# Making the first tile's products one by one, and loading the later weights behind the second input tile

## The chip, the core and the metric

The kernel runs on one core of a Trainium2 chip. The metric is the device time of one execution in microseconds (us). TensorE has no part in this kernel. VectorE (DVE in the profile) makes all products, ScalarE (ACT) issues the loads from its queue, SyncE (SP) issues the stores from its own, and 16 DMA engines move the bytes between HBM and the on-chip memory (SBUF).

## What is computed

Each of 16 x 1024 tokens has a row of 512 numbers and two weights. The output holds the row twice, once times each weight:

```python
batch, seq, hidden = 16, 1024, 512      # k = 2, all float32
x_expanded = x[:, :, np.newaxis, :].repeat(k, axis=2)
weights = expert_weights[..., np.newaxis]
return (x_expanded * weights).astype(np.float32)
```

`expert_indices` is not used. 33.6 MB are read and 67.1 MB are written.

## The kernel before

The 16384 tokens are dealt to 128 partitions, 128 tokens to each. They are cut into tiles of 12 tokens per partition (ten of them, in five groups of two) and a last tile of 8. A full tile is 3.15 MB of input and 6.29 MB of output. Within a group each partition's tokens are consecutive in memory, so a tile's row per partition is one run of 24 KB in and 48 KB out.

*Buffers.* Four input tiles (`XB = 4`) and two output tiles (`bufs=2`) rotate. All weights of the core sit in one tile, `w_tile`, 256 numbers per partition.

*Loads* are issued on ScalarE's queue by `load(i)` (line 80). Tiles 0 to 3 are issued before the main loop, and tile `i + 4` after tile `i` has been worked on (line 129); that load waits until the products that read the buffer are done. Tile 0 comes in three pieces of 4 tokens (line 86). Behind the first piece the weights of the first group are loaded (`first_weights`, line 56); behind the third, all the others (`other_weights`, line 59): one load for groups 1 to 4, cut into 512 runs of 192 bytes, and one for the last group, 128 runs of 64 bytes. Tiles 0 and 1 belong to the first group; tile 2 is the first to need the other weights.

*Products* (line 109) are made on VectorE 4 tokens at a time (`CH = 4`): one `tensor_tensor` multiply of 128 x 4096, with the input broadcast over the two weights and the weights broadcast over the 512 columns. A full tile takes three of them. There are 32 in all.

*Stores* (line 125) are issued on SyncE's queue, one for each tile, when the tile's last product is done. An output buffer is free again when the store two tiles back has landed. There are 11, numbered 0 to 10 below.

A framework orders the instructions and sets the semaphores. Each queue issues in program order.

Of the kernel before, what the change touches and what calls it, by code (L numbers as in the profile page):

```python
# [1 line left out]

# [4 lines left out]


@with_exitstack
def kernel(  # L10
    ctx: ExitStack,
    tc: tile.TileContext,
    x: bass.AP,
    expert_indices: bass.AP,
    expert_weights: bass.AP,
    out: bass.AP,
):
    nc = tc.nc

    batch, seq, hidden = x.shape  # L20
    k = expert_weights.shape[-1]
    P = nc.NUM_PARTITIONS
    ntok = batch * seq
    assert ntok % P == 0
    A_TOTAL = ntok // P

    f32 = mybir.dt.float32
    row = k * hidden
    TX = 12
    TO = 12  # L30
    XB = 4
    CH = 4

    groups = [[12, 12]] * 5 + [[8]]
    assert sum(sum(g) for g in groups) == A_TOTAL

    xf = x.rearrange("b s h -> (b s) h")
    of = out.rearrange("b s k h -> (b s) (k h)")
    wf = expert_weights.rearrange("b s k -> (b s) k")

    w_pool = ctx.enter_context(tc.tile_pool(name="w_pool", bufs=1))
    x_pool = ctx.enter_context(tc.tile_pool(name="x_pool", bufs=XB))
    o_pool = ctx.enter_context(tc.tile_pool(name="o_pool", bufs=2))

    w_tile = w_pool.tile([P, A_TOTAL * k], f32)

    def rows(of_all, done, T):
        return of_all[done * P : (done + T) * P, :].rearrange(
            "(p a) n -> p (a n)", a=T
        )  # L50

    T0 = sum(groups[0])
    G = len([g for g in groups[1:] if sum(g) == T0])
    head = (1 + G) * T0

    def first_weights():
        nc.scalar.dma_start(out=w_tile[:, : T0 * k], in_=rows(wf, 0, T0))

    def other_weights():
        nc.scalar.dma_start(  # L60
            out=w_tile[:, T0 * k : head * k].rearrange("p (g n) -> p g n", g=G),
            in_=wf[T0 * P : head * P, :].rearrange("(g p a) n -> p g (a n)", g=G, p=P),
        )
        nc.scalar.dma_start(
            out=w_tile[:, head * k :], in_=rows(wf, head, A_TOTAL - head)
        )

    tiles = []
    done = 0
    for group in groups:  # L70
        T = sum(group)
        a0 = 0
        for n in group:
            tiles.append((done, T, a0, n))
            a0 += n
        done += T

    loaded = []

    def load(i):  # L80
        if i >= len(tiles):
            return
        done, T, a0, n = tiles[i]
        x_tile = x_pool.tile([P, TX * hidden], f32)
        src = rows(xf, done, T)
        step = TX // 3 if i == 0 else n
        for at in range(0, n, step):
            nc.scalar.dma_start(  # L88
                out=x_tile[:, at * hidden : (at + step) * hidden],
                in_=src[:, (a0 + at) * hidden : (a0 + at + step) * hidden],  # L90
            )
            if i == 0 and at == 0:
                first_weights()
        if i == 0:
            other_weights()
        loaded.append(x_tile)

    for i in range(XB):
        load(i)
    for i, (done, T, a0, n) in enumerate(tiles):  # L100
        x_tile = loaded[i]
        outr = rows(of, done, T)
        for t in range(n):
            if t % TO == 0:
                o_tile = o_pool.tile([P, TO * row], f32)
            if t % CH == 0:
                c = (done + a0 + t) * k
                o = t % TO * row
                nc.vector.tensor_tensor(  # L109
                    out=o_tile[:, o : o + CH * row].rearrange(  # L110
                        "p (t k h) -> p t k h", t=CH, k=k
                    ),
                    in0=x_tile[:, t * hidden : (t + CH) * hidden]
                    .rearrange("p (t h) -> p t h", t=CH)
                    .unsqueeze(2)
                    .to_broadcast([P, CH, k, hidden]),
                    in1=w_tile[:, c : c + CH * k]
                    .rearrange("p (t k) -> p t k", t=CH)
                    .unsqueeze(3)
                    .to_broadcast([P, CH, k, hidden]),  # L120
                    op=mybir.AluOpType.mult,
                )
            if (t + 1) % TO == 0 or t + 1 == n:
                at = t // TO * TO
                nc.sync.dma_start(
                    out=outr[:, (a0 + at) * row : (a0 + t + 1) * row],
                    in_=o_tile[:, : (t + 1 - at) * row],
                )
        load(i + XB)

# [1 line left out]
_INS = ['x', 'expert_indices', 'expert_weights']  # L132
_OUTS = [((16, 1024, 2, 512), 'float32')]


# [23 lines left out]
```

## Time and profile before

| | |
|---|---|
| median of 3 runs | 240.62 us (239.81 to 242.09) |
| the profiled execution | 241.65 us, of which its span is 239.9 us |
| VectorE busy | 139.6 us in 32 products, 4420 ns each on average |
| first load issued, first store issued | 0.73 us, 18.87 us |
| last store issued | 223.67 us |
| a store, from issue to landing | 15.3 to 35.4 us, median 30.5 |
| a tile's load, from issue to landing | median 63.4 us for nine of the full tiles |

How to read it: the profile is one execution. Times count from the start of its span. q1 is the ring of SyncE's queue (stores), q10 that of ScalarE's (loads). A DMA's time "to landing" runs from its issue to the signal that all of its bytes are there, so it includes the time in which it waits behind others in its ring. A share of DMA is that of 16 engines' time; in a short stretch it can show over 1.00, since a packet counts where it starts. A chain of waits is followed back from the last instruction: each step names what released the next.

### The profile page before, as it was taken

Reading aid. Unit: us, or ns where it says so; the run is one execution under the profiler, and the core shown is the slowest. Engines: PE = TensorE matmul, PEld = TensorE weight load, DVE = VectorE, ACT = ScalarE, POOL = GpSimd, SP = SyncE. Lnnn points to the kernel's source line nnn. Section 1 sums busy time; section 2 is a strip of 40 time slices with the busy share of each in tenths; the row PEclk is TensorE's granted clock in tenths of the full one; section 3 lists DMA queues with packets and bytes.
Section 4 is the critical chain, followed back from the end, with each engine's and each line's share of the span. In section 5 each row is a group of like instructions: output and inputs, shape, how many; then the busy total and the mean of one; then the engine's idle time right before and its main releaser. Section 6 shows DMA issues by size and latency. Waiting matters only on the chain.

```text
span 239.9 us, 132 instructions
## 1 busy us (share of the span) xinstructions
DVE 139.6 (58%) x32; POOL 0.2 (0%) x4
## 2 busy tenths in 40 slices
DVE  0999930397079419904970794199049709939200
POOL 0000000000000000000000000000000000000000
DMA  7999999999999999999999999999999999999894
GB/s 254 424 455 365 479 410 406 459 443 389 443 410 512 393 459 393 402 516 393 410 426 418 434 475 393 459 418 467 426 426 410 448 393 481 404 459 459 383 426 186
DMA packets 4272, 100.80 MB, mean 420 GB/s; under 512 B 1200, under 2 KB 1200, under 8 KB 1200
## 3 DMA queue, kind: packets, MB, share of 16 engines
q1 hardware_dynamic: 1584, 67.11, 64.8%
q10 hardware_dynamic: 2688, 33.69, 33.6%
HBM read 33.69 MB, written 67.11 MB: 420 GB/s over the span
## 4 chain that ended last, share of the span: by engine, by line
DMA 61%; DVE 29%; DVEq 2%; issue 0%; ACTq 0%
DMA out_dram<-o_tile 60%; DVE o_tile L109 29%; DMA w_tile<-in_expert_weights_dram 2%; DVEq L154 2%; ACTq L88 0%; DVEq L109 0%
## 5 line engine op out<-in xcount | busy, mean ns | idle before, releaser
L109 DVE TENSOR_TENSOR o_tile<-x_tile,w_tile 128x4096 f32<-128x4096 f32 x32 | 139.6, 4420 | 84.0 <-DMA out_dram<-o_tile 78.3
L143 POOL MEMSET const-bfloat16-1.0<- 128x1 bf16 x1 | 0.1, 102 | 0.0
L143 POOL MEMSET const-uint8-127<- 128x1 uint8 x1 | 0.1, 102 | 0.0
L143 POOL MEMSET const-float32-0.0<- 128x1 f32 x1 | 0.1, 99 | 0.2 <-issue 0.2
L143 POOL MEMSET const-float32-1.0<- 128x1 f32 x1 | 0.1, 99 | 0.0
## 6 DMA issues: line engine op xcount, KB each, us to landing
out_dram<-o_tile SPq DMA_DIRECT2D x10, 6144.0 KB, 30.5
x_tile<-in_x_dram ACTq DMA_DIRECT2D x9, 3072.0 KB, 63.4
out_dram<-o_tile SPq DMA_DIRECT2D x1, 4096.0 KB, 15.3
x_tile<-in_x_dram ACTq DMA_DIRECT2D x3, 1024.0 KB, 6.6
x_tile<-in_x_dram ACTq DMA_DIRECT2D x1, 2048.0 KB, 61.2
w_tile<-in_expert_weights_dram ACTq DMA_DIRECT2D x1, 96.0 KB, 8.6
w_tile<-in_expert_weights_dram ACTq DMA_DIRECT2D x1, 24.0 KB, 4.5
w_tile<-in_expert_weights_dram ACTq DMA_DIRECT2D x1, 8.0 KB, 8.3
```

The costliest lines, as they stand in the source:

```text
L109: nc.vector.tensor_tensor(out=o_tile[:, o : o + CH * row].rearrange("p (t k h) -> p t k h", t=CH, k=k), in0=x_tile[:, t * hidden : (t + CH ...
L143: nc = _bacc.Bacc("TRN2", target_bir_lowering=False, num_devices=1)
L154: with _tile.TileContext(nc) as tc:
```

## The change

A new constant `SINGLES = 1` marks tile 0. For it the wide products are not made; each of its 24 products (12 tokens, two weights) is an instruction of 128 x 512 with the weight as a scalar for each partition. Those whose number leaves 2 when divided by 3, 8 of them, are made on ScalarE, the other 16 on VectorE. All other tiles are as before. And `other_weights()` is called in `load(1)` behind tile 1's load, in place of `load(0)` behind tile 0's third piece.

```diff
+    SINGLES = 1
...
-        if i == 0:
+        if i == 1:
             other_weights()
...
-            if t % CH == 0:
+            for kk in range(k if i < SINGLES else 0):
+                c = (done + a0 + t) * k + kk
+                o = t % TO * row + kk * hidden
+                if c % 3 == 2:
+                    nc.scalar.mul(
+                        out=o_tile[:, o : o + hidden],
+                        in_=x_tile[:, t * hidden : (t + 1) * hidden],
+                        mul=w_tile[:, c : c + 1],
+                    )
+                    continue
+                nc.vector.tensor_scalar(
+                    out=o_tile[:, o : o + hidden],
+                    in0=x_tile[:, t * hidden : (t + 1) * hidden],
+                    scalar1=w_tile[:, c : c + 1],
+                    scalar2=None,
+                    op0=mybir.AluOpType.mult,
+                )
+            if i >= SINGLES and t % CH == 0:
                 c = (done + a0 + t) * k
```

## The prediction

> **What bounds the kernel now.** I read the page's totals and queues first, then the DMA table by stage, then the chain that ended last, and last one steady stretch of the DMA queues.
>
> ```profile
> span 239.9 us, 132 instructions
> DVE 139.6 (58%) x32; POOL 0.2 (0%) x4
> ...
> q1 hardware_dynamic: 1584, 67.11, 64.8%
> q10 hardware_dynamic: 2688, 33.69, 33.6%
> ...
> L109 DVE TENSOR_TENSOR o_tile<-x_tile,w_tile 128x4096 f32<-128x4096 f32 x32 | 139.6, 4420 | 84.0 <-DMA out_dram<-o_tile 78.3
> ```
>
> The stores (q1) and the loads (q10) together fill 98.4% of what 16 DMA engines can carry in the span. VectorE works 58% of it and spends 78.3 us waiting for stores to land. So bytes set the end: 100.8 MB, which the change leaves alone. All that is not covered by transfers is 1.6% of 239.9, or 3.8 us. The table by stage (stretch, its length, VectorE, GpSimd, clock, DMA share, GB/s) shows where that lies:
>
> ```profile
> 0.00:2.00 2.00, 0.00 (x0) 0.20 (x4) 1.00 0.31 53
> 2.00:3.00 1.00, 0.00 (x0) 0.00 (x0) 1.00 0.68 213
> 3.00:6.00 3.00, 0.26 (x1) 0.00 (x0) 1.00 1.01 401
> 6.00:19.00 13.00, 13.00 (x4) 0.00 (x0) 1.00 1.05 437
> 19.00:32.00 13.00, 12.85 (x3) 0.00 (x0) 1.00 1.04 423
> ...
> 147.00:190.00 43.00, 26.03 (x6) 0.00 (x0) 1.00 1.00 434
> ...
> 236.00:238.00 2.00, 0.00 (x0) 0.00 (x0) 1.00 0.31 131
> 238.00:239.90 1.90, 0.00 (x0) 0.00 (x0) 1.00 0.00 0
> ```
>
> Only the first 3 us and the last 4 have free engines. From 3 to 19 us, while no store has been issued, the loads alone already fill them. The chain says the same from the other side: its links are three products (13.11 us) and then a store.
>
> ```profile
> 5.75 13.11 DVE o_tile L109 x3
> ...
> 18.87 26.60 DMA out_dram<-o_tile
> ...
> 45.60 13.11 DVE o_tile L109 x3
> ...
> 58.72 30.48 DMA out_dram<-o_tile
> ...
> 102.45 30.70 DMA out_dram<-o_tile
> ...
> 190.19 24.61 DMA out_dram<-o_tile
> ```
>
> From 58.72 to 102.45 two tiles pass, 21.87 us each; a tile is 3.15 MB in and 6.29 MB out, so 431 GB/s. At that rate a load alone takes 7.3 us and a store 14.6. A store's 30 us are mostly waiting behind the store before it. How the rings share is seen in the DMA queues from 100 to 150 us:
>
> ```profile
> q1 hardware_dynamic: 320, 14.16, 65.5%
> q10 hardware_dynamic: 320, 7.08, 33.0%
> ```
>
> They take turns packet by packet (320 against 320). A store's packet is twice as long, so stores get two thirds of the bytes.
>
> **The change, part by part.**
>
> *The two later weight loads move behind the second tile's load.* ACT's issue of tile 1 comes 0.46 + 0.59 = 1.05 us earlier (2.6 instead of 3.69). Loads 2 and 3 start at 5.49 and 5.86, long after the instruction before them ended, so they don't move. The bytes moved (0.104 MB) take 0.24 us at 431 GB/s: tile 1, which lands at 3.69 + 14.8 = 18.5, would land near 18.2. Tile 2 is the first to need these weights, at 45.6. Cost on the path: nothing, while that cover of 27 us lasts.
>
> *Tile 0's three wide products become 16 on VectorE and 8 on ScalarE.* No row shows a 512-wide product. From above: the wide row's 4418 ns / 8 = 552. From below: the 102 ns of the smallest instruction on the page. I take 552, the same work per element. ScalarE has no row at all; I bound it by 102 and twice 552 and take 552 again, nearest to the same work. The last third of tile 0 lands at 2.10 + 8.7 = 10.8. VectorE then has 5 products left: 5 x 0.552 = 2.76, so tile 0 is done at 13.6 (11.3 with the low price). ScalarE has 3: 12.5; at the double price its 8 products from 6.2 on end at 15.0. The first store is issued at about 13.6 instead of 18.87, 5.3 us earlier. The DVE time saved (13.1 - 16 x 0.552 = 4.3 us) lies beside full DMA engines.
>
> The Trainium skill, "ScalarE: Activation LUTs", section "What ACT_TABLE_LOAD costs", speaks against using ScalarE here: about 2.66 us before a first activation, then an estimated 0.7 us for each of these products. By it, an estimate, ScalarE would start products near 9 and end near 14.6, so the store would go out 1 us later than my sum has it. No run here shows it yet.
>
> *New waits.* SP's first store now waits for two engines; nothing but later stores is queued behind it. On ACT, the load of tile 4 stands behind the 8 products and also waits for VectorE; it went out at 18.88 and would go near 13.6. ACT's ring still holds tiles 1 to 3 then (they land from 18.5 to 55), so nobody waits for it. No load is queued behind the first product that was not so before: loads 0 to 3 are issued ahead of it.
>
> *What an earlier store buys.* The engines are full from 3 us on, so a store that starts 5.3 us earlier takes its bytes from loads. Tile 1 is the first to feel it: between 18.2 and, if the last 3 us of its load alternate with store packets (3 us becomes 9), about 24. Tile 1's products then end between 31.4 and 37. In this time loads 1 to 4 wait in the ring (12.6 MB, 29 us alone), so no engine runs empty. In the steady part each load lands some 11 us before VectorE asks for it (tile 4: 18.88 + 59.0 = 77.9 against 89.3). That cushion shrinks by what stores have gained: 5.3 us x 431 = 2.3 MB at most. Nothing of this shortens the sum of bytes.
>
> *The tail.* Before: store 9 is issued at 211.09 while store 8 lands at 214.80, a lead of 3.7 us; the last store is issued at 223.67 while store 9 lands at 229.3, a lead of 5.6. While both leads hold, the end stays where it is. I take 0 for this, because the last store lands 9.7 us after store 9, its bare bytes at 431, so these leads are enough.
>
> **Sum.** Head 0, products beside full DMA 0, weights 0, tail 0. The profiled execution took 241.65 (span 239.9 plus 1.75 around it), 1.03 over the median of 240.62. On the median: 240.6.
>
> **The rivals.**
>
> *A. The weights get stuck between store packets (chance 0.15).* They are 640 runs, 40 to an engine. With turns taken packet by packet, as at 320 to 320, each could wait for a 1.8 us store packet (14.6 / 8), and tile 2's load stands behind them. If store 0 comes in only as tile 1's load ends, stores 0 and 1 can pass almost alone and tile 2 lands after 50 instead of 33.6. Loads then run ahead later, stores lag, and the stores are alone earlier at the end. There the lead of store 9 falls to 14.6 - 13.25 (landing of one store to issue of the next on its buffer) = 1.4 us. A store's bytes start 0.65 us (first load: issued 0.73, 0.31 of the first 2 us) to 4 us (store 0: no packet from 18.9 to 22) after issue: price 0 to 2.6, so 240.6 to 243.2. Against it: tile 1's 13.1 us of products leave the store ring dry before store 1 comes, and small packets pass at once.
>
> The Trainium skill, "DMA: Bandwidth & Descriptors", section "Queues, rings and completion order", says an engine drains a packet of about 9 to 17 descriptors from one ring before it switches. By that the weights would pass in 3 to 5 turns, an estimated 9 us in place of up to 16 store packets (29 us).
>
> *B. Slower: the loads become the last to arrive at the end (0.13).* If the 2.3 MB that stores gained are never given back, they cost loads 2.3 / 0.144 (a third of 431) = 15.9 us. Tile 10 would land at 146.37 + 61.2 + 15.9 = 223.5 instead of 207.6, its products end at 232.3, and the last store, 9.7 us and some 1.5 of latency, lands at 243.5 instead of 238.95: 245.2. It decides from the point where tile 10 lands more than 214.9 + 5.6 - 1.5 = 219.0. Against it: a late load makes VectorE wait, the store ring runs dry, and the load then has all 431 GB/s (7.3 us instead of 21.9).
>
> *C. The change does not do what it says (0.06):* ScalarE's products take so long that store 0 goes out no earlier: 240.6.
>
> *D. Faster (0.06):* if the whole transfer ran at the 434 of the best long stretch, 100.8 MB take 232.3; with the head's 1.7 and the tail's 3.7 that is 237.7, 2.2 less than the span: 238.4 or, with the scatter of runs, below.
>
> **How the numbers follow.** The main case (0.60) and C stand at 240.6. About 1%, 2.4 us, is what a measurement of this kernel can tell from no change: 238.2 to 243.0. Same: 0.60 + 0.06 + 0.11 of A = 0.77. Slower: B 0.13 + 0.04 of A = 0.17. Faster: 0.06. The range: upwards to A's bound, 243.2; downwards by the 1.5 that the highest run lies over the median, 239.1. Left out are B and D, 0.19.
>
> **What would show it.** Right: the first store issued between 11.5 and 15; DMA share near 1.0 in every stretch from 3 to 234; loads landing later against VectorE than before; stores 9 and 10 issued ahead of the landing before them. Wrong: a stretch in which both rings are empty (A: near 213; B: VectorE waiting for tile 10 past 219), a first load issued later than 0.73, or a different rate in the steady part.

## The result and the profile after

The changed kernel takes 272.25 us (median of 4 runs, 271.97 to 273.2) against 241.11 before: a ratio of 1.130, 95% interval 1.124 to 1.137. The forecast was 240.6, in a range of 239.1 to 243.2. It was wrong by 32 us, and in kind: slower, not the same.

First the page of the changed kernel: its span, the engines' busy time, the queues and the new rows (the last columns are busy us and mean ns of one, then the idle time ahead of it and what ended that).

```profile
span 270.7 us, 155 instructions
...
DVE 133.1 (49%) x45; ACT 6.4 (2%) x9; POOL 0.2 (0%) x4
...
q1 hardware_dynamic: 1584, 67.11, 67.4%
q10 hardware_dynamic: 2688, 33.69, 29.8%
...
L127 DVE TENSOR_TENSOR o_tile<-x_tile,w_tile 128x4096 f32<-128x4096 f32 x29 | 126.6, 4422 | 115.0 <-issue 71.0
L117 DVE TENSOR_SCALAR o_tile<-x_tile,w_tile 128x512 f32<-128x512 f32 x16 | 6.5, 480 | 6.2 <-DMA w_tile<-in_expert_weights_dram 5.8
L111 ACT ACTIVATE o_tile<-x_tile,w_tile 128x512 f32<-128x512 f32 x8 | 5.1, 710 | 0.2 <-DMA x_tile<-in_x_dram 0.2
L111 ACT ACT_TABLE_LOAD x1 | 1.3, 1283 | 5.9 <-DMA x_tile<-in_x_dram 5.9
```

The bytes are the same, and the queues still fill 97.2% of 16 engines, of a span that is 30.8 us longer. So, a few us apart, the DMA engines did not wait for work. They were busy longer with the same work. The stores' ring shows where: 64.8% of 239.9 us was 155 us, 67.4% of 270.7 is 182. The loads' ring stayed at 81 us.

The timeline of the changed kernel (start, length, engine, line, operation, and in brackets the idle time before it) shows a second thing that the forecast did not have:

```profile
10.60 1.95 ACT L111 ACTIVATE o_tile<-x_tile,w_tile 128x512 f32<-128x512 f32 x3 [0.23 <-DMA x_tile<-in_x_dram]
10.60 2.07 DVE L117 TENSOR_SCALAR o_tile<-x_tile,w_tile 128x512 f32<-128x512 f32 x5 [0.36 <-DMA x_tile<-in_x_dram]
18.04 13.10 DVE L127 TENSOR_TENSOR o_tile<-x_tile,w_tile 128x4096 f32<-128x4096 f32 x3 [5.37 <-DMA x_tile<-in_x_dram]
31.16 223.50 SPq L143 DMA_DIRECT2D out_dram<-o_tile  x11
31.17 149.99 ACTq L89 DMA_DIRECT2D x_tile<-in_x_dram  x7
59.55 13.10 DVE L127 TENSOR_TENSOR o_tile<-x_tile,w_tile 128x4096 f32<-128x4096 f32 x3 [28.42 <-issue]
```

Tile 0's products are done on both engines by 12.7, 0.9 us before the forecast's 13.6. But the first store goes out at 31.16, when tile 1's products end. The built program says why (two lines of it, shortened; S[DVE_49] counts VectorE's instructions, S[Activation_49] ScalarE's). The framework put the store of tile 1 ahead of that of tile 0 in SP's queue (`out_set+12288` is tile 1's place in the output):

```
SP DMACopy wait:S[DVE_49]>=19 ...       out=[out_set+12288 ...] in=[o_tile_106_set ...]
...
SP DMACopy wait:S[Activation_49]>=8 ... out=[out_set ...]       in=[o_tile_78_set ...]
```

The trace agrees: of the two issues at 31.16 and 31.65 the first waits for VectorE's semaphore, the second for ScalarE's, whose last update before it came at 12.55. So the first two stores leave together, and with them the loads of tiles 4 and 5, at 31.17 and 31.55.

By stages (stretch, length, VectorE, ScalarE, GpSimd, clock, DMA share, GB/s) the loss of the changed kernel lies here:

```profile
36.00:216.00 180.00, 78.58 (x18) 0.00 (x0) 0.00 (x0) 1.00 1.00 366
216.00:222.00 6.00, 5.62 (x2) 0.00 (x0) 0.00 (x0) 1.00 1.04 451
222.00:234.00 12.00, 10.79 (x3) 0.00 (x0) 0.00 (x0) 1.00 0.59 254
234.00:268.00 34.00, 18.55 (x5) 0.00 (x0) 0.00 (x0) 1.00 1.01 437
```

The kernel before, without the column of ScalarE:

```profile
36.00:206.00 170.00, 99.71 (x23) 0.00 (x0) 1.00 1.00 432
```

For 180 us the engines are full (1.00) and move 366 GB/s where they moved 431 to 432 before. That stretch holds 65.9 MB, which at 431 take 152.9: 27 us lost. From 222 to 234 the share is 0.59: another 5 us of idle engines. Less the microsecond that the rest comes out ahead, this is the 30.8. The idle engines go with drift: the landing signal of a store is 16 updates, one for each engine, and for the store issued at 126.88 the first comes at 151.8 and the last at 167.6; for the store issued at 102.45 in the kernel before they come at 132.2 and 133.2. As soon as the loads are over, at 216, the rate is back at 437 to 451.

The queues between 100 and 150 us give the price of a packet. After:

```profile
DMA packets 553, 18.01 MB, mean 360 GB/s; under 512 B 63, under 2 KB 63, under 8 KB 63
q1 hardware_dynamic: 275, 11.94, 71.7%
q10 hardware_dynamic: 278, 6.07, 28.2%
```

11.94 MB are 243 store packets of 49152 bytes, and 71.7% of 50 us on 16 engines are 574 us: 2.36 us for a packet. Before it was 14.16 MB, 288 packets, 65.5%: 1.82 us. A load packet costs 0.91 to 0.92 us in both. Only stores got slower, by 30%, and only while loads run.

What the two kernels do differently in this stretch is seen in how long the DMAs issued at one moment take to land (KB, us to landing). The kernel before, issued at 58.7:

```profile
out_dram<-o_tile SPq DMA_DIRECT2D x1, 6144.0 KB, 30.5
x_tile<-in_x_dram ACTq DMA_DIRECT2D x1, 3072.0 KB, 63.4
```

The changed kernel, issued at 72.7:

```profile
out_dram<-o_tile SPq DMA_DIRECT2D x1, 6144.0 KB, 41.0
x_tile<-in_x_dram ACTq DMA_DIRECT2D x1, 3072.0 KB, 40.8
```

Before, the load stands behind two others and lands some 11 us away from any store. After, the load and the store that start together end together, 0.2 us apart, and so does each pair up to 216 us. Packets take turns one for one (243 to 247), and load and store both have eight packets on each engine (128 rows on 16 engines), so place by place the load of a partition should run beside the store of the same partition. I call this *in step*. It is the theory that the experiments test.

The kernel before itself took 246.5 to 251.7 us in 4 of its 37 runs on record and 239.7 to 242.3 in the others, so one run of about 250 proves no loss by itself, and where a kernel's runs differ by several per cent they are listed one by one.

### The profile page after: what moved, and what is told of

Same layout as the page of the kernel before. It is cut to its first block, busy times and chain, and to the rows that moved or that the text cites. A ratio compares the mean times of both kernels' runs of the same rounds, so it can differ in the third digit from the quotient of the medians.

```text
span 270.7 us, 155 instructions
## 1 busy us (share of the span) xinstructions
DVE 133.1 (49%) x45; ACT 6.4 (2%) x9; POOL 0.2 (0%) x4
## 3 DMA queue, kind: packets, MB, share of 16 engines
q1 hardware_dynamic: 1584, 67.11, 67.4%
## 4 chain that ended last, share of the span: by engine, by line
DMA 42%; DVE 23%; issue 11%; another core or an unknown queue 5%; DVEq 2%
DMA out_dram<-o_tile 42%; DVE o_tile L127 23%; DVEq L172 2%; DVEq L127 0%
## 5 line engine op out<-in xcount | busy, mean ns | idle before, releaser
L127 DVE TENSOR_TENSOR o_tile<-x_tile,w_tile 128x4096 f32<-128x4096 f32 x29 | 126.6, 4422 | 115.0 <-issue 71.0
L117 DVE TENSOR_SCALAR o_tile<-x_tile,w_tile 128x512 f32<-128x512 f32 x16 | 6.5, 480 | 6.2 <-DMA w_tile<-in_expert_weights_dram 5.8
L111 ACT ACTIVATE o_tile<-x_tile,w_tile 128x512 f32<-128x512 f32 x8 | 5.1, 710 | 0.2 <-DMA x_tile<-in_x_dram 0.2
L111 ACT ACT_TABLE_LOAD x1 | 1.3, 1283 | 5.9 <-DMA x_tile<-in_x_dram 5.9
```

The lines of the kernel that those rows point to most:

```text
L111: nc.scalar.mul(out=o_tile[:, o : o + hidden], in_=x_tile[:, t * hidden : (t + 1) * hidden], mul=w_tile[:, c : c + 1],)
L117: nc.vector.tensor_scalar(out=o_tile[:, o : o + hidden], in0=x_tile[:, t * hidden : (t + 1) * hidden], scalar1=w_tile[:, c : c + 1], scala ...
L127: nc.vector.tensor_tensor(out=o_tile[:, o : o + CH * row].rearrange("p (t k h) -> p t k h", t=CH, k=k), in0=x_tile[:, t * hidden : (t + CH ...
```

## Experiments: which part of the change

**The weights alone.** The edit is the changed line of `load` and nothing else:

```diff
-        if i == 0:
+        if i == 1:
             other_weights()
```

> Theory 1 (the swapped and late first store is the cause): the weight move alone keeps store 0 first, issued near 18.9 us, so the time stays at 240 to 242 and store packets at 1.82 us. Rival (the small weight packets behind tile 1's load hold up the load ring): 245 or more, with loads 2 and 3 landing later than 33.6 and 55.5.

Measured: 241.46 against 241.52 us, ratio 1.001 (0.9988 to 1.0032). Loads 2 and 3 land at 33.4 and 55.4. The weight move alone costs and brings nothing. Store 0 still left at 19.0, so rival A of the prediction, which needs an early store 0, was not put to the test here.

**The small products alone**, with `other_weights()` back in `load(0)`:

> The small products alone, with the later weights left where they were before. Theory (store 0 stands behind store 1 because its products are on two engines, both go out near 31 us, loads and stores run in step): 270 to 274, store packets 2.2 to 2.4 us. Rival (the weight move has a part in the change): 260 or less.

Measured: 273.26 us, one run; store packets 2.39 us between 100 and 150 us (11.75 MB are 239 of them, 71.3% are 570 us). All of the loss is with the small products.

**All 24 small products on VectorE** (`if False:` in place of `if c % 3 == 2:`):

> All 24 small products on VectorE, weights moved. Theory 1: store 0 waits for one engine only, stands first in SP's queue and is issued at 10.7 + 8 x 0.4 = 14 us, before store 1; time 239 to 243, store packets 1.82 us. Rival (an early store that competes with tile 1's load makes the rings slow): 250 or more although store 0 comes first.

Measured: 281.43, 244.84, 281.06 and 280.24 us. Store 0 did go out first, at 15.55, and the time was still lost in three runs of four. My expectation was wrong and its rival came near. In the profiled run (281.43) the load of tile 4, issued at 15.6, took 83.8 us and landed at 99.4; the store of tile 2, issued at 58.3, took 41.3 and landed at 99.6. On the slowest engine load and store are in step again, by another way: the early store took turns from the loads, and these lost their lead (counted in packets started by 45 us, loads were 1.1 tiles ahead of the stores, and 1.7 in the kernel before). Over all engines a store packet cost 2.07 us between 100 and 150 us (11.31 MB are 230 of them, 59.4% are 475 us), less than the 2.36 of the changed kernel. Why one run in four escaped is not known.

```profile
36.00:140.00 104.00, 52.39 (x12) 0.00 (x0) 1.00 1.00 399
140.00:194.00 54.00, 26.19 (x6) 0.00 (x0) 1.00 0.90 352
194.00:240.00 46.00, 19.91 (x5) 0.00 (x0) 1.00 0.77 313
```

In this kernel (same columns, without ScalarE) there is a second loss: shares of 0.90 and 0.77. A store counts as landed only when the last of 16 engines is done, and here the first and the last are 14.7 to 23.3 us apart for the seven stores issued from 58 to 221 us, so some engines are out of work while others finish.

**The changed kernel with the queues in natural order.** An edge without a wait orders tile 1's products behind ScalarE's last product, so that store 0 comes first:

```diff
+                if i == SINGLES:
+                    tc.add_manual_dep(
+                        wide.ins,
+                        last_single.ins.name,
...
```

> The changed kernel, with only the order of the queues mended: tile 1's products are ordered behind ScalarE's last product, so store 0 stands before store 1 and load 4 takes tile 0's buffer. Theory 1: store 0 issued at 12.7 to 13.5, time 239 to 243, some 30 us less than the changed kernel. Rival (ScalarE's products, its table load or the small products themselves slow the rings): 265 to 273 as before.

Measured: 251.53, 262.32, 261.71 and 273.64 us. Store 0 left at 13.53, as the prediction had it. That recovered 0 to 21 us and made the time uncertain. In the profiled run (251.53) tile 1's load landed at 22.4 instead of 18.0, and the rate from 36 to 210 us was 421 to 423 GB/s. So the order of the stores is not the whole cause, and an early store has a price of its own.

Part of that price is rival A of the prediction. With store 0 early, the later weights, which the change put behind tile 1's load, were caught between store packets: from 20 to 32 us the loads' ring moved 111 packets with 0.02 MB in all, the stores' ring 112 with 5.51 MB. The 96 KB of weights took 32.4 us to land instead of 8.6, and tile 2's load, issued at 4.20, landed at 50.1, as rival A has it (size and us to landing, then a piece of the chain that ended last):

```profile
w_tile<-in_expert_weights_dram ACTq DMA_DIRECT2D x1, 96.0 KB, 32.4
4.20 45.90 DMA x_tile<-in_x_dram
```

How much of the 10 us between 251.53 and the kernel before is due to this was not separated.

## Experiments: being in step

**Late in pairs, without the change.** The kernel before, with only store 0 and the load of tile 4 made to wait for tile 1's last product:

```diff
+        ld = load(i + XB)
+        if i == 0:
+            late = [st, ld]
+        if i == 1:
+            for d in late:
+                tc.add_manual_dep(d.ins, wide.ins.name, ...)   # a wait
```

> The kernel before, with store 0 and the load of tile 4 made to wait for tile 1's last product, so that two stores and two loads go out together near 32 us, in natural order, without small products and with the weights where they were. Theory 1 in its first half (starting late and in pairs puts loads and stores in step, and a store packet then takes 2.2 to 2.4 us instead of 1.82): 262 to 273. Rival a (the swap of stores 0 and 1 or the other pairing of buffers is what slows the packets): packets of 1.82 us and 240 to 246. Rival b (ScalarE's work): the same 240 to 246.

Measured: 273.24 us (272.69 to 273.86), ratio 1.132 (1.129 to 1.135). This is the changed kernel's time without one line of the change. No ScalarE, no small product, no swapped store, no other pairing of buffers. From 36 to 216 us:

```profile
36.00:216.00 180.00, 78.58 (x18) 0.00 (x0) 1.00 1.00 364
```

and a store issued at 75.0 lands after 40.0 us, the load beside it after 39.8.

**The same, with the two loads later still.** Tile 1's used input buffer is multiplied by 1.0 in place, three times or once, and loads 4 and 5 wait for that. The stores stay where they were:

```diff
+            for n in range(3):          # 1 in the second kernel
+                idle = nc.vector.tensor_scalar(
+                    out=x_tile[:, :], in0=x_tile[:, :], scalar1=1.0,
+                    scalar2=None, op0=mybir.AluOpType.mult)
+            late.append((ld, 1))
...
+                    idle.ins.name if more else wide.ins.name,
```

> The late pair of stores (273 us) with the loads of tiles 4 and 5 held back by a further 10 us (three idle passes over tile 1's used input buffer), about 3.7 of the 2.7 us turns. Theory 'in step': what slows a store packet is that the load packet of the same place in the tile runs beside it, so a one-time offset of half a tile brings packets back to 1.82 to 1.95 us and the time down to 240 to 255, although more starts late. Rival 'late start' (the time is lost because stores or loads start late): 273 or more. Rival 'short backlog' (loads and stores with little waiting in the rings are slower, whatever their offset): 268 to 285.

Measured: 241.73, 244.63, 250.81 and 249.24 us. The first one has the profile: loads 4 and 5 issued at 42.4 and 42.8, and store packets of 1.82 us in every stretch from 48 us on.

> The same with one idle pass, 3.3 us, about 1.2 turns. Theory 'in step' with the very same partition as the cause: one turn of offset is enough, 240 to 255. If any offset under some turns is slow, packets stay at 2.0 to 2.4 us and the time at 255 to 275. Rival 'late start': 273 to 277.

Measured: 240.67 us (240.5 to 241.05, 8 runs), ratio to before 0.998 (0.996 to 1.001). More work and a later start, and 32 us are back. Its stage from 36 to 190 us, and the store and the load issued at 66.7:

```profile
36.00:190.00 154.00, 85.79 (x20) 0.00 (x0) 1.00 1.01 432
```

```profile
out_dram<-o_tile SPq DMA_DIRECT2D x1, 6144.0 KB, 30.4
x_tile<-in_x_dram ACTq DMA_DIRECT2D x1, 3072.0 KB, 38.6
```

The loads went out at 35.4 and 35.8 instead of 32.1 and 32.5. From then on a load lands 8 us away from the store that started with it, and 432 GB/s hold. The pause of 3.3 us is not made up: the distance is 8.2 us for six pairs in a row. Rival 'late start' is out. With three pauses the landings are only 2.4 to 2.8 us apart for six pairs of the profiled run, and the store packets still take 1.82 us. That three pauses did worse in three of four runs than one is not explained.

**Other addresses in HBM.** The late pair, with the five full groups reading from 517 tokens further on; it computes the products of other tokens:

```diff
-        src = rows(xf, done, T)
+        shift = 517 if T == T0 else 0
+        src = xf[done * P + shift : (done + T) * P + shift, :].rearrange(
+            "(p a) n -> p (a n)", a=T)
```

> The late pair of stores, but the five full groups read their input 517 tokens further on (so the output is that of other tokens); partitions, buffers and packet sizes are as they were, only the HBM addresses of loads against those of stores are others. If the slow packets come from HBM addresses that load and store share in step: 1.82 to 2.0 us and 240 to 258. If they come from the on-chip side (the same partitions read and written in step), or from the pace alone: unchanged, 2.2 to 2.4 us and 270 to 275.

Measured: 273.8 us, ratio 1.136 (1.127 to 1.145); 356 GB/s and store packets of 2.39 us between 100 and 150 us. This shift of HBM addresses changes nothing.

**Other partitions in step.** The late pair, with each load from tile 4 on issued as its even and then its odd partitions:

```diff
+            parts = [slice(0, P)] if i < XB else [slice(0, P, 2), slice(1, P, 2)]
+            ld = [nc.scalar.dma_start(out=x_tile[p, ...], in_=src[p, ...]) for p in parts]
```

> The late pair of stores (273 us, in step), with each load from tile 4 on issued as two, the even partitions and then the odd ones: packets of 24 KB, eight to an engine and the start beside the stores are kept, only the order of partitions within a load is no longer that of the store. Theory 'the same partition read and written in step': packets near 1.82 us and 240 to 255. Rival 'pace alone' (a load and a store that begin together in empty rings are slow, whatever partitions they touch): 2.2 to 2.4 us and 268 to 280.

Measured: 247.43 and 249.77 us, ratio 1.030 (1.017 to 1.042). Where a half of a load and a store were issued together at 68.4, they landed after 29.3 and 29.5 us, so a landing within 0.2 us is not slow by itself:

```profile
36.00:205.00 169.00, 91.67 (x21) 0.00 (x0) 1.00 1.00 425
```

This favours the partition over the pace. Splitting the load also moved its two halves against the store by half a tile, so the rate alone does not tell the two apart. The packets of the trace do better. Since each starts within some nanoseconds of the end of another, they can be strung together engine by engine, and each store packet's place (of eight) compared with that of the load packet just ahead of it. Of 35 such combinations in this kernel the four slowest, at 1.97, 2.03, 2.07 and 2.35 us on average, are those in which both are the same partition, if an engine takes eight consecutive partitions of a store and four of a half load. The other 31 lie between 1.82 and 1.93. In the kernel with three pauses each of the 576 store packets between loads follows the load packet one place further on, and they took 1.82 us: one place is enough. It is not proof, since the trace does not say which partition a packet holds. A load that takes the partitions in another order within one DMA was not tried.

**The changed kernel with one pause.** Everything of the change is kept; the idle pass of 3.3 us stands ahead of the loads of tiles 4 and 5:

> The changed kernel as it is, small products, weights and swapped stores included, with one idle pass of VectorE (3.3 us) ahead of the loads of tiles 4 and 5. If being in step is the whole cause, this alone brings it to 239 to 243 with packets of 1.82 us. If the swap, ScalarE's products or the late stores carry a part of their own, 250 or more stays.

Measured: 250.38, 248.76, 250.09 and 240.12 us. Most of the 31 us is back with nothing of the change undone, and all of it in one run; the other three miss the 239 to 243 that I expected. In the profiled run (250.38) the rate is 424 from 36 to 194 us; what is left is a stretch of idle engines behind it:

```profile
36.00:194.00 158.00, 79.50 (x19) 0.00 (x0) 0.00 (x0) 1.00 1.00 424
194.00:216.00 22.00, 19.38 (x5) 0.00 (x0) 0.00 (x0) 1.00 0.71 305
216.00:246.00 30.00, 14.65 (x4) 0.00 (x0) 0.00 (x0) 1.00 0.99 428
```

The landings are 5.5 us apart (33.0 and 38.5 for the pair issued at 69.0), and a store packet cost 1.84 us between 100 and 150 us (13.37 MB are 272, 62.7% are 502 us). The engines had drifted by 5.7 to 9.0 us on the stores issued from 69 to 186 us. So the loads and stores are out of step, and what this run loses is lost otherwise; why is not shown.

**Three input buffers in the kernel before** (`XB = 3`):

> The kernel before with three input buffers in place of four; store 0 goes out first at 18.9 as before, no small products. A load then starts with less waiting in its ring, so loads and stores begin closer together: if being in step is the cause, landings of loads and stores fall within 1 us of each other and the time goes to 255 to 280; if the landings stay more than 3 us apart, 240 to 246. Rival (what matters is only the late or swapped first store): 240 to 246 in any case.

Measured: 241.65 and 249.49 us. In the profiled run (241.65) the pair issued at 58.8 lands after 30.3 and 41.1 us, 11 us apart, and the packets cost 1.82 us. So it was not the fourth buffer that kept the kernel before out of step.

## Why the prediction was wrong

*Right:* the head and the small products cost nothing on the path. The products took 0.48 and 0.71 us against 0.552 for each; tile 0 was done at 12.7 against 13.6. The weight move alone is worth 0 (ratio 1.001). The DMA engines set the end, but by the time that each packet took, not by the bytes alone. Three readings were off without weight in the sum: the weights moved are 0.106 MB, not 0.104; loads 2 and 3 did move, to 4.26 and 5.53; and of the 30.5 us of the store issued at 58.72, 8.6 pass behind the store before it, which lands at 67.3, and 21.9 are its own turns with the loads.

*The first step that failed* is "The first store is issued at about 13.6 instead of 18.87". The products were ready, the store was not issued: it stood behind tile 1's store and left at 31.65. I took SP's queue to keep the order of the text and wrote that nothing but later stores was queued behind it. But the queues are ordered when the program is built, and with tile 0's products on two engines the framework put the other store first. Rival C ("store 0 goes out no earlier") named the event, for another reason (slow products on ScalarE), and priced it at nothing.

*The step that cost the time* is "At that rate a load alone takes 7.3 us and a store 14.6", with 431 GB/s taken as a property of the queues. It is a property of how loads and stores lie against each other: 432 GB/s out of step, 364 to 366 in step. A store took 8 x 1.82 = 14.6 us before and takes 8 x 2.36 = 18.9. In the sum ("products beside full DMA 0") every delay of a store or a load was free as long as some ring had work; the late pair shows that a delay of 13 us costs 32 with the engines full up to 216 us, and the kernel with one pause that the same delay of the stores, out of step, costs nothing.

*Rival B* foresaw that an early store lets the loads arrive last. That happened where the store really was early (the 24 products on VectorE, the mended order), and at up to 281 us. It was priced by the tail alone, at 4.6 us (245.2 less 240.6). In the profiled run of the 24 products on VectorE the loads also fell into step with the stores on the slowest engine.

*Rival A* had no occasion in the changed kernel, whose first store was late. Where store 0 was early and the weights moved, in the mended order, it came about as described: tile 2 landed at 50.1.

*The tail* was taken as 0. From 222 to 234 us idle engines cost 5 us in the changed kernel, whose engines had drifted apart by up to 15.7 us.

*On the pages of the skill:* the Trainium skill, "ScalarE: Activation LUTs", section "What ACT_TABLE_LOAD costs", has the table load at 1283 ns, which the trace shows to the nanosecond. The drain of 1.4 us that it adds is not seen: the load starts at 5.90 and the first ACTIVATE at 7.19. The Trainium skill, "DMA: Bandwidth & Descriptors", section "Queues, rings and completion order", lets an engine drain some 9 to 17 descriptors before it switches rings; the rows of before and after (320 to 320, 243 to 247 data packets) fit turns of one packet of 24 or 48 KB. For small packets the measurement differs from the page: in the mended order 111 of the weights' packets went by against 112 store packets, one by one, and the 9 us that the prediction estimated by the page for their passing became a landing after 32.4 us. The measurement decides.

*What stays open:* which part of the chip slows a store that runs beside the load of its own partition. HBM addresses are unlikely after the shifted rows, the partition is likely after the even and odd ones and their packets, and neither is settled. Nor is it known why the engines drift apart more in some runs than in others. No version ran clearly faster than the kernel before; the best, the late pair with one pause, is the same at 0.998.

## What to carry to other kernels

Where two rings fill the DMA engines, bytes over rate is a forecast only as long as loads and stores keep their distance: look at when the pairs issued together land. For tiles like these 0.2 us apart, pair after pair, was the slow case, and 2.4 us or more ran at full speed. A change of the first tile can set that distance for the whole run. Small loads queued ahead of large ones can be held up packet by packet once a store runs. And before pricing an earlier store, look up its place in its queue in the built program: work put on a second engine can move it behind the next tile's.

## What the runs showed of the hardware

With the same bytes, the same packet sizes and full engines, a 48 KB store packet took 1.82 us or 2.36 us, and a 24 KB load packet 0.92 us in both cases. A single pause of 3.3 us at 32 us decided between 273.2 and 240.7 us for the whole kernel. Packets of 192 bytes took turns one by one with store packets of 48 KB (111 to 112 in 12 us), so 96 KB of weights needed 32.4 us to land.
